# Larger scratch writes for the split state-space operands and a later, spread-out load of small inputs in a two-layer hybrid decoder

## The chip, the cores and the metric

The program runs on one core of one Trainium2 chip. The core has a matrix engine (PE; its weight loads are shown as PEld), a vector engine (DVE), an activation engine (ACT), a general engine (POOL) and a queue engine (SP); 16 DMA engines move data for all of them. DMAs are issued here from SP (weights, output) and from POOL (all else). The metric is the device time of one execution in microseconds (us).

## The reference

Two decoder layers over 256 tokens of width 2048, all in float32. Cut to what matters here:

```python
for l in range(2):
    q, k, v, u = x @ w_in[...]                # u: 1024 wide, 64 groups of 16
    attn = diff_attention(rope(q), rope(k), v)
    # state space: bu = einsum('blgh,gph->blgp', u, bb), complex, 64 states a group
    # scanned over the tokens; y = Re(C s) + D u; g = gelu(y); g * sigmoid(g @ w_glu)
    ssm = s5_ssm(u, ...)
    merged = sigmoid(x @ w_ga) * (attn @ w_attn_up) + sigmoid(x @ w_gs) * (ssm @ w_ssm_up)
    x = layer_norm(alpha * x + merged @ w_out)
    x = layer_norm(alpha * x + relu(x @ w_up)**2 @ w_down)
```

## The kernel before

Each float32 product is made of reduced-precision products. An operand is split into hi (a rounded copy, ACT, L142) and lo (the rest, DVE, L144), and PE adds hi·hi, hi·lo and lo·hi. Weights are streamed: SP loads one chunk of 128x1024 numbers (512 KB) into one of four buffers (L344), ACT and DVE split it into one of three hi/lo buffers, PE consumes it. `gemm_feat` (L536) uses 24 matmuls of 256 columns a chunk, `gemm_tok` (L480) 12 of 512 columns.

A layer goes: u (two `gemm_feat` of 8 chunks each), q, k, v, the gates, `w_attn_up`, GLU (`w_glu`), `w_ssm_up`, `w_out`, layer norm, MLP, layer norm. Beside this foreground a background of generators is advanced: after each chunk `bg.pump(rate[0])` adds credit (about microseconds of DVE work) and runs generator steps until it is spent. In layer 0 the background first runs `rope_gen` (rotary tables), `b_gen(0)` (state-space parameters and the split of B), then `ssm_gen`, and later attention beside it. For layer 1, `b_gen(1)` runs in layer 0's MLP through `ahead_gen`. `bg.finish(sgen)` (L995) runs whatever is left before GLU. A scheduler then orders the instructions of each engine by a simulated timeline; each engine takes its own in that order.

Two helpers tie POOL's DMAs to PE: a DMA in `drip` is issued one a chunk, behind the chunk's last matmul (L460); `hold` (L454) keeps an instruction behind the latest chunk.

The state space's input product needs B and u split and stacked on partitions. Both go through scratch in DRAM: `b_gen` writes hi, lo, hi for each of four groups (L606, 12 writes of 256 KB a layer into `bsplit`), `u_evac` writes hi, hi, lo of each pair of column tiles (L950, 12 writes of 256 KB a layer into `usplit`). `operands` (L674) reads them back, 96 partitions each, two DMAs a set, 16 sets a layer; there is one buffer each (`bs`, `us`), so a set's DMAs wait until PE has done the matmuls of the set before (L702). Six DVE operations follow on each set, and after four sets of a group come scan, output product `y` (L748), GELU.

The seven small inputs are loaded by POOL at the very start (L180 to L192). The last layer norm's reciprocal root for the second half of the tokens runs on POOL (L852).

Of the kernel before, what the change touches and what calls it, by code (L numbers as in the profile page):

```python
# [30 lines left out]
L = 64  # L31
NCH = S // L
# [8 lines left out]
RATE = (2.0, 1.8)  # L41
# [3 lines left out]
LEAD = 3  # L45
# [59 lines left out]
def trunk(ctx: ExitStack, tc: tile.TileContext, A, out):  # L105
    nc = tc.nc
    V, SC, GP, PE = nc.vector, nc.scalar, nc.gpsimd, nc.tensor
# [5 lines left out]
    tmp = ctx.enter_context(tc.tile_pool(name="tmp", bufs=1))  # L113
# [62 lines left out]
    dram = ctx.enter_context(tc.tile_pool(name="dram", bufs=1, space=bass.MemoryType.DRAM))  # L176
    xkeep = A["x"].rearrange("(t p) d -> t p d", p=P)
    x = [None, None]
    prm = slot([P, 3, 64], name="prm")
    GP.dma_start(prm, A["ssm_p"])  # L180
    pos_i = t_bg([P, S]).bitcast(I32)
    GP.dma_start(pos_i, A["pos"][None, :].broadcast_to([P, S]))
    inv = const([P, 2], "inv")
    GP.dma_start(inv, A["inv"])
    lnp = const([P, DEPTH, 2, 2, NKT], "lnp")
    GP.dma_start(lnp, A["lnp"])
    dsk = const([P, DEPTH, 8], "dsk")
# [215 lines left out]
    rate = [RATE[0]]  # L403
    wts = {}

    def weights(key, l, *idx):
        k = (key, l) + idx
        if k not in wts:
            wts[k] = A[key][(l,) + idx]
        return wts[k]  # L410

    for l in range(DEPTH):
# [11 lines left out]
        for key, *idx in order:  # L424
            w = weights(key, l, *idx)
# [3 lines left out]
    for c in range(4):  # L429
        raw = wpool.tile([P, 4, 256], F32, tag="w", name=nm("xraw"), bufs=RAW_BUFS)  # L430
        t = slot([P, 4, 2, 256], F32R, "xT")
        xT.append(t)
        parts = [slice(0, 2), slice(2, 4)] if c == 0 else [slice(0, 4)]
        for i, k in enumerate(parts):
            nc.sync.dma_start(raw[:, k], A["xT"][c][:, k])
            split(t[:, k, 0, :], t[:, k, 1, :], raw[:, k])
            if c + i < LEAD:
# [151 lines left out]
    def b_gen(l):  # L589


        raw = slot([P, 4, 2, 256], name="braw")
        for g in range(4):
            hold(GP.dma_start(raw[:, g], A["bT"][l][:, g]))
            yield 0.3
        if l == 0:
            yield from ssm_param_gen()
        else:
            yield 2.0
        bsplit[l] = dram.tile([4, 4, 3, 32, 2, 256], F32, tag=f"bsplit{l}", name=f"bsplit{l}")  # L600
        hi, lo = (slot([P, 4, 2, 256], name="bhl") for _ in range(2))
        for g in range(4):
            h = SC.activation(hi[:, g].bitcast(F32R), raw[:, g], AF.Copy)
            hold(h)
            V.tensor_tensor(lo[:, g].bitcast(F32R), raw[:, g], hi[:, g], op=ALU.subtract)
# [54 lines left out]
    def ssm_gen(l, st):  # L660
        lp = l * 32
        e_re = slot([P, 4, 8, L], name="e_re")
        e_im = slot([P, 4, 8, L], name="e_im")
        w = [slot([P, NCH, 8, L], name="sw") for _ in range(2)]
        for g in range(4):
            if l in emem:
                for t, e in zip((e_re, e_im), emem[l]):
                    drip.append((t[:, g], e[:, g]))
            else:
                for step in e_steps(l, g, e_im[:, g], e_re[:, g]):  # L670
                    yield 0.1 if isinstance(step, tuple) else step
        while st["u"] is None:
            yield 0.5
        def operands(i):  # L674
            if i == 16:
                return None
            g, h, kk = i // 4, i // 2 % 2, i % 2
            bs = tmp.tile([96, 2, 2, P], F32, tag="bs", name=nm("bs"), bufs=1)
            GP.dma_start(bs.rearrange("p q c s -> p q (c s)"), bsplit[l][g, 2 * kk:2 * kk + 2, :, :, h].rearrange("q m r s -> (m r) q s"))
            us = tmp.tile([96, 2, 256], F32, tag="us", name=nm("us"), bufs=1)  # L680
            GP.dma_start(us, st["split"][2 * kk:2 * kk + 2, :, :, 2 * g + h].rearrange("q m r t -> (m r) q t"))
            return bs, us

        nxt = operands(0)
        uT = st["u"]
        for g in range(4):
            jj = slice(lp + 8 * g, lp + 8 * g + 8)
            cz = tmp.tile([P, 2, 8, 32], F32, tag="cz", name=nm("cz"), bufs=2)
            GP.dma_start(cz, cmem[l][g] if l in cmem else A["cT"][l, g])
# [7 lines left out]
            for k in range(4):  # L697
                bs, us = nxt
                bu = psa.tile([P, 2, 2, NCH, L], F32, tag="bu", name=nm("bu"), bufs=1)
                for q in range(2):  # L700
                    for ri in range(2):
                        PE.matmul(bu[:, q, ri].rearrange("p a b -> p (a b)"), bs[:, q, ri, :].bitcast(F32R), us[:, q, :].bitcast(F32R), start=True, stop=True)  # L702
                nxt = operands(4 * g + k + 1)
                yield 0.3
                er = e_re[:, g, 2 * k:2 * k + 2, None, :].broadcast_to([P, 2, NCH, L])
                ei = e_im[:, g, 2 * k:2 * k + 2, None, :].broadcast_to([P, 2, NCH, L])
                wr, wi = (w[ri][:, :, 2 * k:2 * k + 2, :].rearrange("p c q t -> p q c t") for ri in range(2))
# [214 lines left out]

        return evac

    prep = [rope_gen(), b_gen(0)]
    first = True

    for l in range(DEPTH):
# [112 lines left out]
        norms = {}  # L1041
# [154 lines left out]
```

## Time and profile before

| | |
|---|---|
| Median of 3 runs | 2718.39 us (2705.3 to 2719.93) |
| Profiled execution, its own time | 2716.07 us |
| Its span | 2714.1 us |
| DVE, ACT, POOL busy | 70%, 48%, 5% |
| Mean granted PE clock | 0.992 of full speed |
| Moved by DMA | 535.76 MB, mean 197 GB/s |

Busy time is per engine over the span. "Idle before, releaser" says how long the engine waited ahead of an instruction and for whom. An "x" behind a busy time counts instructions; a few per cent of the matmul records can be missing. The granted clock is a share of PE's 2.4 GHz.

### The profile page before, as it was taken

To read this page: it belongs to the slowest core of one execution; us is meant where nothing else is said; L and a number is where in the kernel's file an instruction comes from. 1 tells how busy PE (TensorE), PEld (TensorE's weight loads), DVE (VectorE), ACT (ScalarE), POOL (GpSimd) and SP (SyncE) were. 2 spreads that over 40 slices of the span, in tenths; PEclk is the share of its full clock that TensorE was granted. 3 is DMA by queue.
4 is the path that set the end of the run, shared out by engine and by line. 5 is a ranking of instruction groups with operands and counts; after the bars stand their busy time and mean duration, and the time that the engine had idled before them with its cause. 6 is when DMAs were issued, how large, how long until landed. Compare 5 with 4: busy or idle time off the path is not lost. (4 is left out here: it accounts for less than half of the span.)

```text
span 2714.1 us, 37124 instructions
## 1 busy us (share of the span) xinstructions
PE 2648.8 (98%) x14144; PEld 2254.0 (83%) x14144; DVE 1906.6 (70%) x2675; ACT 1307.5 (48%) x1755; POOL 147.1 (5%) x274
## 2 busy tenths in 40 slices
PE   6999999999999999999998999999999999999998
PEld 6988877888888878888898987778888888888886
DVE  6899998666765566665656999987776655656556
ACT  4555555444554454443443655544445544435442
POOL 2100000000000010000012000001000000000000
PEclk9999999999999999999999999999999999999999
DMA  8756655674656677666657566557746666665673
GB/s 267 214 181 188 191 180 170 217 238 129 214 188 193 200 231 216 219 201 194 233 172 229 180 187 190 177 159 230 259 134 207 188 194 189 192 194 186 194 242 131
DMA packets 158659, 535.76 MB, mean 197 GB/s; under 512 B 27505, under 2 KB 27537, under 8 KB 158481
## 3 DMA queue, kind: packets, MB, share of 16 engines
q1 hardware_dynamic: 133344, 482.40, 56.1%
q0 software_dynamic: 25136, 50.99, 6.6%
q8 instruction: 111, 1.82, 0.3%
q14 instruction: 68, 0.55, 0.1%
HBM read 513.32 MB, written 19.92 MB: 196 GB/s over the span
## 5 line engine op out<-in xcount | busy, mean ns | idle before, releaser
L144 DVE TENSOR_TENSOR wlo<-w,whi 128x1024 fp32r<-128x1024 f32 (+1 forms) x884 | 1077.2, 1220 | 648.0 <-ACT whi L142 643.4
L142 ACT ACTIVATE whi<-w 128x1024 fp32r<-128x1024 f32 (+1 forms) x884 | 934.4, 1058 | 1073.8 <-PE g L478 649.9
L572 PE MATMUL g<-xT,whi 128*128 128x512 f32 x1920 | 656.3, 395 | 3.3 <-ACT whi L142 3.3
L572 PE MATMUL g<-xT,wlo 128*128 128x256 f32 x1920 | 497.9, 280 | 1.5 <-DVE wlo L144 1.5
L572 PEld LDWEIGHTS g<-xT,whi 128*128 128x128 f32 x1920 | 345.1, 188 | 68.2 <-ACT whi L142 3.9
L572 PEld LDWEIGHTS g<-xT,wlo 128*128 128x128 f32 x1920 | 362.2, 189 | 23.1 <-DVE wlo L144 2.8
L475 PE MATMUL g<-wlo,hT 128*128 128x512 f32 x972 | 378.2, 389 | 0.0
L474 PE MATMUL g<-whi,hT 128*128 128x512 f32 x972 | 378.2, 389 | 0.0
L478 PE MATMUL g<-whi,hT 128*128 128x512 f32 x972 | 299.1, 389 | 0.0
L475 PE MATMUL g<-wlo,xT 128*128 128x512 f32 x680 | 267.7, 394 | 0.5 <-DVE wlo L144 0.5
L474 PE MATMUL g<-whi,xT 128*128 128x512 f32 x680 | 265.5, 392 | 0.0
L549 PE MATMUL g<-xT,whi 128*128 128x256 f32 x768 | 218.6, 288 | 18.1 <-ACT whi L142 18.1
L551 PE MATMUL g<-xT,wlo 128*128 128x256 f32 x768 | 213.9, 289 | 5.6 <-DVE wlo L144 5.5
L550 PE MATMUL g<-xT,whi 128*128 128x256 f32 x768 | 218.1, 287 | 0.0
L475 PEld LDWEIGHTS g<-wlo,hT 128*128 128x128 f32 x972 | 182.5, 188 | 38.0
L474 PEld LDWEIGHTS g<-whi,hT 128*128 128x128 f32 x972 | 182.4, 188 | 37.9
L478 PEld LDWEIGHTS g<-whi,hT 128*128 128x128 f32 x972 | 182.4, 188 | 37.8
L478 PE MATMUL g<-whi,xT 128*128 128x512 f32 x680 | 211.5, 391 | 0.0
L549 PEld LDWEIGHTS g<-xT,whi 128*128 128x128 f32 x768 | 150.7, 196 | 19.1 <-ACT whi L142 19.0
L551 PEld LDWEIGHTS g<-xT,wlo 128*128 128x128 f32 x768 | 147.4, 197 | 7.8 <-DVE wlo L144 7.5
L550 PEld LDWEIGHTS g<-xT,whi 128*128 128x128 f32 x768 | 150.9, 197 | 0.0
L475 PEld LDWEIGHTS g<-wlo,xT 128*128 128x128 f32 x680 | 128.0, 188 | 27.3 <-issue 1.2
(292 smaller groups left out, 3162.9 us busy)
## 6 DMA issues: line engine op xcount, KB each, us to landing
w<-in_w_in_dram SPq DMA_DIRECT2D x253, 512.0 KB, 3.7
w<-in_w_mlp_down_dram SPq DMA_DIRECT2D x243, 512.0 KB, 3.5
w<-in_w_mlp_up_dram SPq DMA_DIRECT2D x240, 512.0 KB, 3.6
w<-in_w_out_dram SPq DMA_DIRECT2D x54, 512.0 KB, 4.5
w<-in_w_attn_up_dram SPq DMA_DIRECT2D x32, 512.0 KB, 3.6
w<-in_w_ssm_up_dram SPq DMA_DIRECT2D x32, 512.0 KB, 3.8
w<-in_w_glu_dram SPq DMA_DIRECT2D x16, 512.0 KB, 3.6
lnb<-in_ln_dram POOLq DMA_DIRECT2D x32, 256.0 KB, 4.1
```

Of the source, the lines that this page charges most:

```text
L142: SC.activation(hi, src, AF.Copy, scale=scale)
L144: V.tensor_tensor(lo, src, hi.bitcast(F32), op=ALU.subtract)
L474: mm(PE.matmul(ps[tt], act(kt)[:, 0, ts], hi[:, k, :], start=kt == 0, stop=False))
L475: mm(PE.matmul(ps[tt], act(kt)[:, 0, ts], lo[:, k, :], start=False, stop=False))
L478: mm(PE.matmul(ps[tt], act(kt)[:, 1, ts], hi[:, k, :], start=False, stop=kt == nkt - 1))
L549: m(PE.matmul(o, wh, ah, start=first and b % 2 == 0, stop=False))
L550: m(PE.matmul(o, wh, al, start=False, stop=False))
L551: m(PE.matmul(o, wl, ah, start=False, stop=last and b % 2 == 1))
L572: mm[j](PE.matmul(o, wt, mv, start=kt == 0 and i == 0, stop=last and i == 1))
```

## The change

The scratch gets another layout. B's hi and lo of two groups are gathered in one tile and written by one DMA of 1 MB (two a layer), and so are u's hi and lo of one `gemm_feat` (two a layer). The three stacked copies are no longer made in DRAM: `operands` reads 128 partitions (both of B's parts against both of u's, so lo·lo is added too), by four DMAs of 64 partitions a set, with B's rows repeated in the read. A set now holds another pair of the group's eight tiles (`k::4`).

The small inputs go into `drip`: one behind each of the first chunks. The first x tile is loaded in three pieces. `b_gen(0)` comes ahead of `rope_gen` and pauses for 4.0 credit; the rate is 1.2 instead of 2.0 in the two u products of layer 0. C's tiles are loaded one group ahead and under `hold`. The last layer norm's reciprocal root goes to DVE.

```diff
-    GP.dma_start(prm, A["ssm_p"])
...
-    GP.dma_start(lqk.rearrange("p a b c d -> p (a b c d)"), A["lqk"][None, :].broadcast_to([P, DEPTH * 4 * QK]))
...
-        parts = [slice(0, 2), slice(2, 4)] if c == 0 else [slice(0, 4)]
+        parts = [slice(0, 1), slice(1, 2), slice(2, 4)] if c == 0 else [slice(0, 4)]
...
-    drip = []
+    drip = [(prm, A["ssm_p"]), (pos_i, A["pos"][None, :].broadcast_to([P, S])), (inv, A["inv"]),
+            (lqk.rearrange("p a b c d -> p (a b c d)"), A["lqk"][None, :].broadcast_to([P, DEPTH * 4 * QK])),
+            (dsk, A["dsk"]), (sub, A["sub"]), (lnp, A["lnp"])]
...
+        if l == 0:
+            yield 4.0
...
-        hi, lo = (slot([P, 4, 2, 256], name="bhl") for _ in range(2))
-        for g in range(4):
...
-            for m, t in enumerate((hi, lo, hi)):
-                GP.dma_start(bsplit[l][g, :, m], t[:, g])
-            yield 0.6
+        bsplit[l] = [dram.tile([4, 32, 2, 2, 2, 256], F32, tag=f"bsplit{l}{i}", name=f"bsplit{l}{i}") for i in range(2)]
+        for i in range(2):
+            hl = slot([P, 2, 2, 2, 256], name="bhl")
...
+            GP.dma_start(bsplit[l][i].rearrange("j r m k h c -> (j r) (m k h c)"), hl.rearrange("p m k h c -> p (m k h c)"))
...
-            GP.dma_start(bs.rearrange("p q c s -> p q (c s)"), bsplit[l][g, 2 * kk:2 * kk + 2, :, :, h].rearrange("q m r s -> (m r) q s"))
-            GP.dma_start(us, st["split"][2 * kk:2 * kk + 2, :, :, 2 * g + h].rearrange("q m r t -> (m r) q t"))
+            for m in range(2):
+                ms = slice(64 * m, 64 * m + 64)
+                GP.dma_start(bs[ms].rearrange("p h c s -> p (h c s)"), b[m][:, None].broadcast_to([32, 2, 512]))
+                GP.dma_start(us[ms].rearrange("p h t -> p (h t)"), u)
...
-    prep = [rope_gen(), b_gen(0)]
+    prep = [b_gen(0), rope_gen()]
...
-            for m, t in enumerate((hi, hi, lo)):
-                GP.dma_start(st["split"][:, m, :, ct:ct + 2], t)
+            if b == 1:
+                GP.dma_start(st["split"][n].rearrange("j r m c t -> (j r) (m c t)"), uhl[n].rearrange("p m c t -> p (m c t)"))
...
+            rate[0] = 1.2 if l == n == 0 else RATE[l]
...
-                            lambda tt, vd: ln_stats(tt, stats, norms, vd, tt == 1))
+                            lambda tt, vd: ln_stats(tt, stats, norms, vd, tt == 1 and nxt is not None))
```

On POOL, in layer 0's u products, the order before was this (`bhl` and `uhl` are the split tiles, `bs` and `us` the operands of the state space's product):

```order
L594 DMA braw_317<-in_bT_dram 128x512 x4
L607 DMA bsplit_506<-bhl_507 4x32x512 x2
L607 DMA bsplit_506<-bhl_508 4x32x512
L951 DMA usplit_170<-uhl_168 4x32x512 x2
L607 DMA bsplit_506<-bhl_507 4x32x512 x2
L951 DMA usplit_170<-uhl_168 4x32x512 x2
L951 DMA usplit_170<-uhl_169 4x32x512
L607 DMA bsplit_506<-bhl_507 4x32x512 x4
```

After the change, at the same place on POOL:

```order
L459 DMA lnp<-in_lnp_dram 128x128
L959 DMA usplit_166<-uhl_164 128x2048
L604 DMA bsplit_538<-bhl_540 128x2048
L689 DMA us_1019<-usplit_166 64x512 x2
L604 DMA bsplit_539<-bhl_576 128x2048
L688 DMA bs_1018<-bsplit_538 64x1x512 x2
L959 DMA usplit_167<-uhl_165 128x2048
L688 DMA bs_1072<-bsplit_538 64x1x512
L689 DMA us_1073<-usplit_166 64x512
```

Four writes led by 128 partitions stand where 24 led by a dimension of 4 stood, and a set of operands takes four DMAs.

On PE, the output product `y` of layer 0's last group stood among the matmuls of `w_attn_up` (`ahl` is the attention's result), with some 12 chunks of it still to come:

```order
L478 MATMUL g_4546<-whi_4527,ahl_2593 128x512 x2
L748 MATMUL y_4257<-sw_605,cz_3728 32x256 x4
L474 MATMUL g_4545<-whi_4549,ahl_2593 128x512
L748 MATMUL y_4257<-sw_606,cz_3728 32x256 x4
L748 MATMUL y_4257<-sw_605,cz_3728 32x256 x4
L748 MATMUL y_4257<-sw_606,cz_3728 32x256 x4
L475 MATMUL g_4545<-wlo_4550,ahl_2593 128x512
```

After the change the same product stands within GLU (`ghl` is GELU's result split; `ghl_4790` its first half, which the last group doesn't touch):

```order
L546 MATMUL g_4798<-ghl_4790,wlo_4803 128x256
L756 MATMUL y_4368<-sw_745,cz_2659 32x256 x4
L544 MATMUL g_4799<-ghl_4790,whi_4802 128x256
L545 MATMUL g_4799<-ghl_4790,whi_4802 128x256
L546 MATMUL g_4799<-ghl_4790,wlo_4803 128x256
L544 MATMUL g_4799<-ghl_4790,whi_4802 128x256
L545 MATMUL g_4799<-ghl_4790,whi_4802 128x256
L546 MATMUL g_4799<-ghl_4790,wlo_4803 128x256
L756 MATMUL y_4368<-sw_746,cz_2659 32x256 x4
L756 MATMUL y_4368<-sw_745,cz_2659 32x256 x4
L756 MATMUL y_4368<-sw_746,cz_2659 32x256 x4
```

So the state space of layer 0 ends some 190 matmuls later in PE's order. Behind this piece PE has 28 more matmuls on the first half before the first one that reads the second.

## Rows read from the trace of the kernel before

**Rows 1.** The page: busy time of PE, and its busy tenths in 40 slices.

```profile
PE 2648.8 (98%) x14144; PEld 2254.0 (83%) x14144; DVE 1906.6 (70%) x2675; ACT 1307.5 (48%) x1755; POOL 147.1 (5%) x274
...
PE   6999999999999999999998999999999999999998
```

**Rows 2.** Busy time by stretch: PE, PEld, DVE, ACT, POOL, clock, DMA share, GB/s.

```profile
0.00:30.00 30.00, 19.03 (x131) 17.33 (x132) 19.34 (x49) 15.32 (x17) 9.05 (x24) 1.00 0.86 282
10.00:20.00 10.00, 6.58 (x48) 5.77 (x48) 7.29 (x14) 5.82 (x7) 0.00 (x0) 1.00 0.92 316
30.00:50.00 20.00, 20.00 (x168) 20.00 (x168) 19.44 (x67) 11.72 (x17) 6.25 (x9) 1.00 0.86 251
50.00:100.00 50.00, 35.29 (x251) 34.54 (x250) 28.09 (x46) 20.00 (x27) 13.13 (x20) 0.83 0.84 247
...
100.00:450.00 350.00, 347.39 (x1981) 291.41 (x1980) 336.21 (x575) 190.11 (x322) 19.64 (x35) 1.00 0.60 184
1430.00:1470.00 40.00, 30.57 (x231) 30.22 (x231) 20.29 (x24) 13.24 (x16) 9.68 (x15) 0.87 0.80 244
...
960.00:990.00 30.00, 25.18 (x129) 20.57 (x128) 19.93 (x28) 17.42 (x26) 4.32 (x7) 0.94 0.82 242
```

**Rows 3.** Waits, 0 to 115 us: total us, times, longest.

```profile
ACT whi L142 <- DMA w<-in_w_in_dram: 30.5, 11, 13.1
...
PE g L551 <- DVE wlo L144: 3.5, 4, 1.9
```

**Rows 4.** Waits, 1425 to 1475 us (layer 1's u products).

```profile
ACT whi L142 <- DMA w<-in_w_in_dram: 20.5, 4, 11.0
...
PE bu L702 <- DMA us<-usplit: 9.4, 2, 7.8
```

**Rows 5.** DMA issues of the whole span: count, KB each, median us to landing.

```profile
bsplit<-bhl POOLq DMA_DIRECT2D x24, 256.0 KB, 15.1
usplit<-uhl POOLq DMA_DIRECT2D x24, 256.0 KB, 12.5
bs<-bsplit POOLq DMA_DIRECT2D x32, 192.0 KB, 4.3
...
emem<-ss POOLq DMA_DIRECT2D x8, 256.0 KB, 4.4
xkeep<-x POOLq DMA_DIRECT2D x8, 256.0 KB, 10.5
...
cz<-in_cT_dram POOLq DMA_DIRECT2D x4, 256.0 KB, 7.2
...
lqk<-in_lqk_dram POOLq DMA_DIRECT2D x1, 256.0 KB, 7.8
ss<-in_pos_dram POOLq DMA_DIRECT2D x1, 128.0 KB, 7.1
```

**Rows 6.** Tile bs: ns min, median, max of an issue on POOL.

```profile
L679 POOL DMA_DIRECT2D bs<-bsplit x32: 637/640/674, 70.6 to 1738.6; - x32
```

**Rows 7.** Chain of waits near the end: start, us, two 512-column matmuls.

```profile
2641.90 0.45 PE g L478 x2
```

**Rows 8.** Timeline around layer 0's last `y`: start, us, instruction (DVE, then ACT).

```profile
443.46 0.68 DVE L737 TENSOR_TENSOR sw<-sw,ss 128x512 f32<-128x512 f32 x1
...
448.22 0.69 DVE L755 TENSOR_TENSOR ss<-y,ss 128x512 f32<-128x512 f32 x1
...
453.25 1.22 DVE L146 SCALAR_TENSOR_TENSOR ghl<-uT,ghl 128x1024 fp32r<-128x1024 f32 x1
...
451.95 1.07 ACT L142 ACTIVATE ghl<-uT 128x1024 fp32r<-128x1024 f32 x1
```

**Rows 9.** DVE timeline of the last layer norm.

```profile
2692.11 0.16 DVE L854 TENSOR_TENSOR rsp<-rstd 128x1 f32<-128x1 f32 x1
...
2694.07 2.73 DVE L1127 SCALAR_TENSOR_TENSOR x<-x,mv,lnb 128x512 f32<-128x512 f32 x4
...
2707.80 2.74 DVE L1129 SCALAR_TENSOR_TENSOR x<-x,rstd,lnb 128x512 f32<-128x512 f32 x4 [2.20 <-POOL rstd L856]
```

More of the change, by code (lines that the diff above doesn't have):

```diff
@@ L436, in trunk @@
             split(t[:, k, 0, :], t[:, k, 1, :], raw[:, k])
-            if c + i < LEAD:
+            if (c, i) in ((0, 0), (0, 2), (1, 0), (2, 0)):
                 load_next(c == i == 0)
@@ L599, in b_gen @@
             yield 2.0
-        bsplit[l] = dram.tile([4, 4, 3, 32, 2, 256], F32, tag=f"bsplit{l}", name=f"bsplit{l}")
-        hi, lo = (slot([P, 4, 2, 256], name="bhl") for _ in range(2))
-        for g in range(4):
-            h = SC.activation(hi[:, g].bitcast(F32R), raw[:, g], AF.Copy)
-            hold(h)
-            V.tensor_tensor(lo[:, g].bitcast(F32R), raw[:, g], hi[:, g], op=ALU.subtract)
-            for m, t in enumerate((hi, lo, hi)):
-                GP.dma_start(bsplit[l][g, :, m], t[:, g])
-            yield 0.6
+        bsplit[l] = [dram.tile([4, 32, 2, 2, 2, 256], F32, tag=f"bsplit{l}{i}", name=f"bsplit{l}{i}") for i in range(2)]
+        for i in range(2):
+            hl = slot([P, 2, 2, 2, 256], name="bhl")
+            for k in range(2):
+                hold(SC.activation(hl[:, 0, k].bitcast(F32R), raw[:, 2 * i + k], AF.Copy))
+                V.tensor_tensor(hl[:, 1, k].bitcast(F32R), raw[:, 2 * i + k], hl[:, 0, k], op=ALU.subtract)
+                yield 0.6
+            GP.dma_start(bsplit[l][i].rearrange("j r m k h c -> (j r) (m k h c)"), hl.rearrange("p m k h c -> p (m k h c)"))
     def e_steps(l, g, im, re, hold=lambda i: i):
@@ L664, in ssm_gen, with load_c @@
         w = [slot([P, NCH, 8, L], name="sw") for _ in range(2)]
+        def load_c(g):
+            cz = tmp.tile([P, 2, 8, 32], F32, tag="cz", name=nm("cz"), bufs=2)
+            hold(GP.dma_start(cz, cmem[l][g] if l in cmem else A["cT"][l, g]))
+            return cz
         for g in range(4):
@@ L671, in ssm_gen @@
                     yield 0.1 if isinstance(step, tuple) else step
+        cz_next = load_c(0)
         while st["u"] is None:
@@ L676, in operands @@
                 return None
-            g, h, kk = i // 4, i // 2 % 2, i % 2
-            bs = tmp.tile([96, 2, 2, P], F32, tag="bs", name=nm("bs"), bufs=1)
-            GP.dma_start(bs.rearrange("p q c s -> p q (c s)"), bsplit[l][g, 2 * kk:2 * kk + 2, :, :, h].rearrange("q m r s -> (m r) q s"))
-            us = tmp.tile([96, 2, 256], F32, tag="us", name=nm("us"), bufs=1)
-            GP.dma_start(us, st["split"][2 * kk:2 * kk + 2, :, :, 2 * g + h].rearrange("q m r t -> (m r) q t"))
+            g, j = i // 4, i % 4
+            bs = tmp.tile([P, 2, 2, P], F32, tag="bs", name=nm("bs"), bufs=1)
+            us = tmp.tile([P, 2, 256], F32, tag="us", name=nm("us"), bufs=1)
+            b = bsplit[l][g // 2][j, :, :, g % 2].rearrange("r m h c -> m r (h c)")
+            u = st["split"][g // 2][j, :, :, 2 * (g % 2):2 * (g % 2) + 2].rearrange("r m h t -> (r m) (h t)")
+            for m in range(2):
+                ms = slice(64 * m, 64 * m + 64)
+                GP.dma_start(bs[ms].rearrange("p h c s -> p (h c s)"), b[m][:, None].broadcast_to([32, 2, 512]))
+                GP.dma_start(us[ms].rearrange("p h t -> p (h t)"), u)
             return bs, us
@@ L687, in ssm_gen @@
             jj = slice(lp + 8 * g, lp + 8 * g + 8)
-            cz = tmp.tile([P, 2, 8, 32], F32, tag="cz", name=nm("cz"), bufs=2)
-            GP.dma_start(cz, cmem[l][g] if l in cmem else A["cT"][l, g])
+            cz = cz_next
+            cz_next = load_c(g + 1) if g < 3 else None
             rt = t_bg([P, 8, L])
@@ L704, in ssm_gen @@
                 yield 0.3
-                er = e_re[:, g, 2 * k:2 * k + 2, None, :].broadcast_to([P, 2, NCH, L])
-                ei = e_im[:, g, 2 * k:2 * k + 2, None, :].broadcast_to([P, 2, NCH, L])
-                wr, wi = (w[ri][:, :, 2 * k:2 * k + 2, :].rearrange("p c q t -> p q c t") for ri in range(2))
+                er = e_re[:, g, k::4, None, :].broadcast_to([P, 2, NCH, L])
+                ei = e_im[:, g, k::4, None, :].broadcast_to([P, 2, NCH, L])
+                wr, wi = (w[ri][:, :, k::4, :].rearrange("p c q t -> p q c t") for ri in range(2))
                 ta, tb = t_bg([P, 2, NCH, L]), t_bg([P, 2, NCH, L])
@@ L940, in trunk @@
         uT = slot([P, 8, 256], name="uT")
-        uhl = [slot([P, 8, 256], name="uhl") for _ in range(2)]
-        st["split"] = dram.tile([4, 3, 32, 8, 256], F32, tag=f"usplit{l}", name=f"usplit{l}")
+        uhl = [slot([P, 2, 4, 256], name="uhl") for _ in range(2)]
+        st["split"] = [dram.tile([4, 32, 2, 4, 256], F32, tag=f"usplit{l}{i}", name=f"usplit{l}{i}") for i in range(2)]
         def u_evac(b, ps):
@@ L946, in u_evac @@
             u = uT[:, ct:ct + 2, :]
-            hi, lo = (t[:, ct:ct + 2, :] for t in uhl)
+            hi, lo = (uhl[n][:, m, 2 * b:2 * b + 2] for m in range(2))
             SC.activation(u, ps, AF.Copy)
             split(hi.bitcast(F32R), lo.bitcast(F32R), u)
-            for m, t in enumerate((hi, hi, lo)):
-                GP.dma_start(st["split"][:, m, :, ct:ct + 2], t)
+            if b == 1:
+                GP.dma_start(st["split"][n].rearrange("j r m c t -> (j r) (m c t)"), uhl[n].rearrange("p m c t -> p (m c t)"))
         rate[0] = RATE[l]
```

5 lines of the change are left out of this document (removed).

## The prediction

> **What bounds the kernel now.** I read the page's busy line and slices first, then busy time by stretch, the waits of the bad stretches, the DMA issues, and two pieces of the timeline. The reader is to see in [rows 1] that PE is busy 2648.8 of 2714.1 us: all waiting together is 65 us, 2.4%, and the first slice is the worst (6 where nearly all others have 9). The change leaves the matmuls as many as they were, so it can win only waits and what a lowered clock costs.
>
> [rows 2] say where. At full pace PE starts 168 matmuls in 20 us (30:50), 8.4 a us. Counted by that, 0:30 with 131 lost 30 - 15.6 = 14.4 us; 50:100 with 251 lost 20.1 us, part of it waiting, part at a granted clock of 0.83; in layer 1, 1430:1470 with 231 lost 12.5 us (clock 0.87). In layer 0's MLP, 960:990 was idle 4.8 us, and the clock of 0.94 costs 25.2 x 0.06 = 1.5 us more: 6.3 us. These four stretches hold 53 us. From 100 to 450 us PE lacks 2.6 us only, with DVE at 96%.
>
> The waits name the weights' transfers: in the first 115 us ACT waits 30.5 us for them, 13.1 at once [rows 3], and in layer 1 20.5 us, beside 9.4 us that PE waits for `us` read back from scratch [rows 4]. In just these stretches POOL sends the split parts. Their 256 KB take 15.1 and 12.5 us to land at the median, where `emem`, as large and also written to DRAM, takes 4.4 [rows 5].
>
> Two readings fit. `emem` is led by 128 partitions, the split parts by a dimension of 4, so they may use few engines; or they are merely written in a crowd: `xkeep`, led by 128 too, takes 10.5 us amid `usplit` [rows 5]. The Trainium skill ("DMA: Bandwidth & Descriptors", on why a DMA increments its semaphore by 16) says that a DMA runs on the largest number of engines up to 16 that divides the slowest dimension of both sides: 4 before, 16 now. The ratio 15.1 to 4.4 agrees, 10.5 for `xkeep` warns that part of it is crowding. By this rule alone the writes' stalls would all go, by crowding alone only the bytes count; the sums below stand without it.
>
> **The change part by part.**
>
> *Start.* Before, the small inputs and two C tiles go out with the first weights: `lqk` and `pos`, the two largest of seven, and two of `cz` are 896 KB, 0.92 MB [rows 5]. At 316 GB/s, the best 10 us shown [rows 2], they take 2.9 us, in a stretch in which PE lives from hand to mouth. Behind the first products they compete with weights still, but later. The lower rate and the pause take DVE work away from the weights' lo parts, for which PE waited 3.5 us [rows 3]; I count 2.6 of it. Together -5.5 us; bounds: -1 (all returns as the same bytes a little later) and -9.
>
> *Writes in layer 0.* 24 writes of 256 KB, 6.3 MB, become four of 1 MB, 4.2 MB. What is left of the 20.1 us? A chunk is 0.524 MB for 24 matmuls, 2.86 us, so the weights want 183 GB/s. With 4.2 MB of writes, 1.0 MB for the first two operand sets and 0.5 MB of C over some 45 us, 127 GB/s come on top: 310 GB/s. That is just below the best of 316; 30:50 shows 251. At 280 in between, 1.4 MB come late, 5 us; with a bit for the second C tile and the inputs moved here I leave 5.6 us: -14.5. Bounds: at 247 GB/s (50:100) 2.8 MB are late, 11.5 us, -8.5; all gone, -20.
>
> *Writes in layer 1.* One 256 KB transfer a chunk (the tables `e_re`, `e_im` and `xkeep`) stays. 12.5 us at 244 GB/s are 3.0 MB late; 1.05 MB fewer are written, 4.3 us. If the even deal gives half of the rest too, -8.5. Bounds -4 and -12.5.
>
> *Writes in layer 0's MLP.* Likewise 1.05 MB fewer at 242 GB/s is 4.3 us of the 6.3; -4.5, bounds -1 and -6.3.
>
> *Operand reads.* Each of 32 sets now takes four DMAs and 512 KB for two and 384 KB. 4.2 MB more lie in stretches where the DMA share is 0.60 [rows 2]: nothing. The latency counts more. An issue of 96 partitions costs 0.64 us [rows 6]; four of 64 partitions are not shown, at most 4 x 0.64 = 2.6 us, at least the 1.3 us of now; I take 2.2. With 4.3 us to land [rows 5] a set comes 6.5 us after the matmuls before it. In PE's new order the fewest matmuls between two sets are 36 of 512 columns, at 0.225 us each [rows 7] 8.1 us. The order before left as few as 24 such, 5.4 us against 1.3 + 4.3 = 5.6, and outside the crowded stretches PE hardly waited. Cost 0. If that cover is gone, PE waits with all weights' matmuls queued behind it; priced as a rival. The Trainium skill ("DMA: Bandwidth & Descriptors", "Rules for kernel authors") speaks against the split in halves: two transfers to disjoint partition halves serialize, and one of 128 partitions should be used. By it halves win no time over whole transfers; no run so far shows it, and the sum stays as it is, since it counts all four.
>
> *Later end of the state space.* The wider sets and the lower rate put layer 0's last `y` within GLU. Before, from the end of the last DVE step ahead of it (443.46 + 0.68) to the second half of `ghl` (453.25 + 1.22) went 10.3 us [rows 8], hidden under `w_attn_up`. Now 28 matmuls of 256 columns, 3.3 us, lie between, so PE can stand 7.0 us. Without the wait ahead of it, from 448.22 to ACT's part at 453.02 is 4.8 us, 1.5 uncovered. Between the two, nearer the longer, since three weight splits stand in between on DVE: +4.5. Bounds +1 and +10 (DVE some us late besides).
>
> *Tail.* POOL's part goes, for which DVE idled 2.20 us; nine DVE instructions take its place, 2694.07 - 2692.11 = 1.96 us in the first half [rows 9]. The four independent steps no longer run beside it: -0.2 us, bounds -0.3 and +0.3.
>
> *The rest.* The stride `k::4` and the two parts side by side leave every DVE and PE instruction its size; `rope_gen` behind `b_gen` is needed only at q. Nothing.
>
> Sum: -5.5 - 14.5 - 8.5 - 4.5 + 4.5 - 0.2 = -28.7. From the profiled execution's 2716.07 that is 2687.4; that execution lies 2.3 us under the median of 2718.39, so I say 2688.
>
> **The rivals.**
>
> *Only bytes count* (the crowd, not the deal). For: `xkeep`'s 10.5 us, 0.84 DMA share in 50:100. Against: 247 GB/s there is less than 316. Then layer 0 wins 2.1 MB less 0.5 of wider sets, 1.6 MB at 247, 6.5 us; layer 1 4.3, MLP 4.3, start 2.9; with GLU's 4.5 back that is -13.5: 2704.
>
> *DVE becomes the bound of layer 0.* DVE has 96% in 100:450; PE arriving 20 us sooner at GLU may find the state space undone. For: `y` ends in GLU now. Against: DVE idled 20 us of 50:100 and 10 of 0:30, and can use them too. If three quarters of layer 0's 20 us return, 2703.
>
> *Operands late (slower).* At every set within a group, 24 of 32, PE waits in its order for the fourth DMA. It decides once a set lands later than 8.1 us after the set before. If the four take turns and the last lands at 10 us instead of 6.5, each costs 1.9 us, 46 us: 2688 + 46 = 2734. Against: the median landing is 4.3 us even with the crowd in it.
>
> *The change doesn't act*: the writes still run on few engines. The destination is led by 128 now, as `emem`'s; I give it nothing of its own, it would end like the first rival.
>
> **How the numbers follow.** Forecast 0.68 (its own range 2674 to 2702), bytes only 0.17, DVE 0.09, operands late 0.06. A change of under 0.5%, 13.6 us, can't be told from none with this kernel, whose three runs differ by 14.6; the line is at 2704.8. Faster: 0.67 of the first, 0.10 of the second, 0.05 of the third, 0.82. Same: 0.01, 0.07, 0.04, 0.01: 0.13. Slower 0.05. All good bounds at once give 2718.4 - 47.1 = 2671, all bad ones 2718.4 - 4.2 = 2714, which leaves out the slower rival; 8 in 10 I put from 2671 to 2709.
>
> **What would show it.** 50:100 with over 370 matmuls, not 251, and a clock near 1.0; 0:30 with over 165. The four large writes land in under 10 us each, and no wait of ACT for `w` is over 5 us there; with waits over 5 us the first rival is right. 1430:1470 over 300 matmuls. A new wait of PE at GLU, 3 to 7 us, at some 460 us; over 12 us says DVE. PE waiting for `us` or `bs` at many sets of 200 to 450 us says the slower rival, and it would prove me wrong outright; so would no change of the stall in 50:100.

## The result and the profile after

The changed kernel takes 2682.70 us (median of 4 runs, 2679.49 to 2684.72), the kernel before in the same session 2712.07 (4 runs); the ratio is 0.989, 95% interval 0.9864 to 0.9915. The forecast was 2688, its range 2671 to 2709. The profiled execution took 2682.85 us, its span is 2681.1, 33.0 shorter than before's; the profiled execution of before was 4 us above the later median, so differences of the two profiles come out some 4 us larger than those of the medians.

The page of the profile after: PE's busy line and its slices.

```profile
PE 2642.8 (99%) x14144; PEld 2250.5 (84%) x14144; DVE 1909.8 (71%) x2685; ACT 1308.3 (49%) x1756; POOL 139.4 (5%) x289
...
PE   8999999999999999999999999999999999999998
```

All of PE's waiting is now 38 us, not 65 [rows 1], and the first slice is an 8, not a 6.

Busy time by stretch after (PE, PEld, DVE, ACT, POOL, clock, DMA share, GB/s), against [rows 2]:

```profile
0.00:30.00 30.00, 22.98 (x162) 22.17 (x163) 16.32 (x25) 14.60 (x16) 7.21 (x21) 1.00 0.87 289
...
50.00:100.00 50.00, 50.00 (x419) 50.00 (x418) 44.99 (x89) 32.06 (x42) 4.98 (x10) 1.00 0.79 262
100.00:450.00 350.00, 344.40 (x1844) 285.10 (x1843) 325.25 (x550) 183.23 (x311) 31.92 (x63) 1.00 0.62 187
...
960.00:990.00 30.00, 30.00 (x165) 25.91 (x164) 22.20 (x29) 18.39 (x26) 0.94 (x2) 1.00 0.64 198
1430.00:1470.00 40.00, 39.16 (x326) 38.96 (x326) 38.97 (x56) 23.00 (x29) 4.47 (x10) 1.00 0.59 187
```

Three of the four bad stretches are full or nearly so at a clock of 1.00: 419 matmuls for 251, 165 for 129, 326 for 231. 0:30 has 162 for 131. The work of the last two comes some 18 and 26 us earlier in the changed kernel, so the like stretches there are these, and they are as full (174 and 332 matmuls):

```profile
942.00:972.00 30.00, 30.00 (x174) 26.19 (x174) 21.99 (x28) 18.25 (x24) 1.66 (x3) 1.00 0.76 247
1404.00:1444.00 40.00, 39.80 (x332) 39.57 (x331) 31.93 (x43) 20.62 (x25) 10.82 (x22) 1.00 0.88 270
```

The DMA issues after (count, KB each, median us to landing), against [rows 5]:

```profile
us<-usplit POOLq DMA_DIRECT2D x64, 128.0 KB, 4.9
bs<-bsplit POOLq DMA_DIRECT2D x64, 128.0 KB, 4.7
...
usplit<-uhl POOLq DMA_DIRECT2D x4, 1024.0 KB, 6.3
bsplit<-bhl POOLq DMA_DIRECT2D x4, 1024.0 KB, 6.6
...
xkeep<-x POOLq DMA_DIRECT2D x8, 256.0 KB, 6.2
```

1 MB lands in 6.3 and 6.6 us where 256 KB took 12.5 and 15.1. `xkeep`, which was not changed, went from 10.5 to 6.2. It lies beside the split writes; run 1 below (few bytes, uneven writes) has 8.5 for it and run 2 (the bytes of before, even writes) 7.1, so both play a part, and the uneven deal the larger one.

The largest wait for weights in the first 115 us, against [rows 3] (total, times, longest):

```profile
ACT whi L142 <- DMA w<-in_w_in_dram: 12.6, 11, 3.2
```

12.6 us for 30.5, and none over 3.2. In layer 1's u products [rows 4] ACT no longer waits for `w` at all. Of the signs that the forecast named, three were missed: 0:30 has 162 matmuls and not over 165, one of the four writes of layer 0 took 10.2 us and not under 10, and the new wait in GLU is 1.5 us and not 3 to 7 (its rows are shown further down).

### The profile page after: what moved, and what is told of

Its sections match the earlier page's. It is cut to its first block, busy times and chain, and to the rows that moved or that the text cites. A ratio compares the mean times of both kernels' runs of the same rounds, so it can differ in the third digit from the quotient of the medians.

```text
span 2681.1 us, 37176 instructions
## 1 busy us (share of the span) xinstructions
PE 2642.8 (99%) x14144; PEld 2250.5 (84%) x14144; DVE 1909.8 (71%) x2685; ACT 1308.3 (49%) x1756; POOL 139.4 (5%) x289
## 5 line engine op out<-in xcount | busy, mean ns | idle before, releaser
L567 PEld LDWEIGHTS g<-xT,whi 128*128 128x128 f32 x1920 | 344.4, 188 | 64.1
L567 PEld LDWEIGHTS g<-xT,wlo 128*128 128x128 f32 x1920 | 361.5, 188 | 20.8 <-DVE wlo L144 0.3
L544 PEld LDWEIGHTS g<-xT,whi 128*128 128x128 f32 x768 | 149.0, 194 | 6.1 <-ACT whi L142 6.0
L469 PEld LDWEIGHTS g<-whi,xT 128*128 128x128 f32 x680 | 128.4, 189 | 27.0 <-ACT whi L142 2.1
L473 PEld LDWEIGHTS g<-whi,xT 128*128 128x128 f32 x680 | 127.4, 188 | 27.1 <-issue 0.4
```

What stands on the lines that cost most here:

```text
L469: mm(PE.matmul(ps[tt], act(kt)[:, 0, ts], hi[:, k, :], start=kt == 0, stop=False))
L473: mm(PE.matmul(ps[tt], act(kt)[:, 1, ts], hi[:, k, :], start=False, stop=kt == nkt - 1))
L544: m(PE.matmul(o, wh, ah, start=first and b % 2 == 0, stop=False))
L567: mm[j](PE.matmul(o, wt, mv, start=kt == 0 and i == 0, stop=last and i == 1))
```

## The experiments

Each run was timed in five rounds; the kernel before had 2711.1, 2710.2 and 2711.9 us beside the three groups of runs. Four marks will do for most of them, read from the tiles' first starts: the matmuls of the first 100 us, the first matmul on `ahl` (`w_attn_up`, attention's result) and on `sgl` (`w_ssm_up`, behind GLU: the end of layer 0's mixer but for its output products), and the span. The first shows the transfers, `ahl` to `sgl` the end of attention and of the state space. The mark `ahl` is not quite the same place everywhere: from it to `sgl` PE does 430 matmuls before, 421 or 422 in the changed kernel and in runs 1, 2, 6, 11 and 12, 440 in run 5, 447 or 448 in runs 4, 7 and 9, and 460 or 461 in runs 3, 8 and 10, where more of attention's matmuls come behind the first on `ahl`.

| kernel | matmuls to 100 us | DVE busy to 100 us | `ahl` | `sgl` | span | median us |
|---|---|---|---|---|---|---|
| before | 546 | 66.9 | 432.8 | 505.8 | 2714.1 | 2711 |
| changed | 745 | 81.2 | 414.4 | 488.1 | 2681.1 | 2682.7 |
| 1 uneven | 618 | 67.8 | 426.4 | 500.1 | 2716.6 | 2719.9 |
| 2 small even, spare copies | 742 | 80.9 | 412.3 | 486.1 | 2677.5 | 2680.7 |
| 3 start alone | 591 | 67.4 | 424.2 | 512.2 | 2709.0 | 2718.1 |
| 4 writes alone | 666 | 82.6 | 417.9 | 503.8 | 2696.4 | 2697.2 |
| 5 full rate, no pause | 723 | 80.8 | 416.3 | 495.6 | 2686.4 | 2692.2 |
| 6 `us` by one DMA, led by 2 | 722 | 78.7 | 455.3 | 528.6 | 2776.6 | 2777.8 |
| 7 writes alone, late `y` | 684 | 83.5 | 415.6 | 502.7 | 2695.0 | 2698.7 |
| 8 start alone, late `y` | 612 | 67.9 | 422.7 | 516.5 | 2715.3 | 2723.0 |
| 9 writes alone, DVE later | 666 | 82.2 | 417.6 | 496.0 | 2689.2 | 2690.3 |
| 10 start alone, DVE later | 600 | 67.5 | 423.6 | 520.0 | 2715.4 | 2723.1 |
| 11 `us` by one DMA, led by 64 | 739 | 80.6 | 412.7 | 484.8 | 2684.5 | 2685.2 |
| 12 pieces of 256 KB | 734 | 79.7 | 415.0 | 488.7 | 2683.9 | 2685.3 |

The profiled execution of run 3 was the shortest of its twelve, 2711.2 us, so its row shows less loss than its median. Those of runs 5, 8 and 10 too were the shortest, 4 to 6 us under their medians.

**The deal or the bytes (runs 1 and 2).** Run 1 takes the even deal away and keeps everything else:

```diff
-        bsplit[l] = [dram.tile([4, 32, 2, 2, 2, 256], ...
+        bsplit[l] = [dram.tile([4, 33, 2, 2, 2, 256], ...
-            GP.dma_start(bsplit[l][i].rearrange("j r m k h c -> (j r) (m k h c)"), ...
+            GP.dma_start(bsplit[l][i][:, :32].rearrange("j r m k h c -> j r (m k h c)"), ...
```

> The changed kernel with one thing altered: the scratch of each split part has 33 rows in place of 32 in its second dimension, so that the same eight writes of 1 MB are led by a dimension of 4 again and not by 128. Bytes, count and order stay. Theory (the even deal over the engines is what frees the weights' transfers): the large writes land in over 20 us instead of 6.3, the weights wait again in 50:100, in layer 0's MLP and around 1430:1470, and over two thirds of the gain goes: 2703 to 2725 us. Rival (only the bytes and the count of writes matter): within 4 us of the changed kernel's 2682.7, that is 2679 to 2687.

Measured: 2719.9 us, ratio to before 1.003 (1.0018 to 1.0042), as the theory had it. All of the gain is gone. The issues and two stretches of run 1:

```profile
usplit<-uhl POOLq DMA_DIRECT2D x4, 1024.0 KB, 20.3
bsplit<-bhl POOLq DMA_DIRECT2D x4, 1024.0 KB, 19.5
...
xkeep<-x POOLq DMA_DIRECT2D x8, 256.0 KB, 8.5
```

```profile
50.00:100.00 50.00, 42.06 (x323) 41.00 (x322) 34.95 (x82) 22.45 (x32) 6.92 (x12) 0.93 0.75 248
...
1430.00:1470.00 40.00, 27.59 (x199) 27.24 (x198) 22.00 (x28) 12.06 (x14) 11.27 (x21) 0.83 0.73 234
```

The same bytes land three times as late, and the stall at 1430:1470 is larger than before the change (199 matmuls for 231). Not all of it is the weights': in 1425:1475 PE waits 12.4 us for `us`, which is read back behind the late writes (9.4 before the change [rows 4]). Run 2 keeps the deal and gives the bytes and the count back:

```diff
-            GP.dma_start(bsplit[l][i].rearrange("j r m k h c -> (j r) (m k h c)"), ...
+                for m in range(2):
+                    GP.dma_start(bsplit[l][i][:, :, m, k].rearrange("j r h c -> (j r) (h c)"), ...
+                GP.dma_start(bspare[:, 2 * i + k], hl[:, 0, k].rearrange("p h c -> p (h c)"))
```

> The changed kernel with its eight writes of 1 MB made 48 of 256 KB, each led by 128 partitions; of every six pieces two go to a spare scratch that nobody reads, so that bytes and count are those of the kernel before and only the deal is the new one. Theory (the deal decides): nearly all of the gain stays, 2682 to 2690 us, 50:100 with over 390 matmuls. Rival (bytes and count decide): the 4.2 MB more cost what my sum took for them, 6.5 us in layer 0 and 4.3 each in layer 1 and in the MLP, 2696 to 2700 us, with 50:100 under 370 matmuls.

Measured: 2680.7 us, ratio 0.9888 (0.9875 to 0.9901), as the changed kernel and 1.3 us below the theory's range. Its 50:100:

```profile
50.00:100.00 50.00, 49.90 (x416) 49.69 (x415) 45.08 (x93) 31.78 (x42) 10.58 (x20) 1.00 0.88 301
```

So the DMAs moved 301 GB/s there, some 2.0 MB more than in the changed kernel, and PE didn't notice. The rival that only bytes count is out: what bytes and count cost is too little to be seen here, and the deal costs the whole gain.

**The start and the writes apart (runs 3 and 4).** Run 3 is the kernel before with `drip`, x in three pieces, pause, rate and order of the changed one; run 4 is the changed kernel without these:

```diff
+    GP.dma_start(prm, A["ssm_p"])
...
-        if l == 0:
-            yield 4.0
...
-    prep = [b_gen(0), rope_gen()]
+    prep = [rope_gen(), b_gen(0)]
...
-            rate[0] = 1.2 if l == n == 0 else RATE[l]
```

> The kernel before with the start part alone: the small inputs one by one behind the first products, x in three pieces at first, the pause, the lower rate in the first product and the B preparation ahead of the rotary tables; writes, scratch and operand reads stay those of before. Theory (the start is worth about 5.5 us by itself, and the crowd behind it stays): 2704 to 2709 us, 0:30 with over 155 matmuls, not 131. Rival (what the start wins is lost again in the crowd of uneven writes that follows): 0:30 as full, but 50:100 with fewer than 251 matmuls and the whole at 2710 to 2716 us.

> The changed kernel with the start part undone (small inputs sent with the first weights, the usual rate, no pause, the old order of the two preparations); the large writes, the wider operand sets and the C tiles one group ahead stay. Theory (start and writes add up): 2686 to 2691 us, 0:30 with some 130 matmuls, 50:100 with over 390. Rival (the start wins nothing in the end, since the state space sets the time at GLU): 2680 to 2684 us.

Measured: the start alone 2718.1 us, ratio 1.0026 (1.0014 to 1.0037), 7 us slower than before; the writes alone 2697.2, ratio 0.9944 (0.9932 to 0.9956). All four ranges were missed, both theories and both rivals. The parts don't add up: the start loses 7 us by itself and is worth 14.5 (2697.2 - 2682.7) on top of the even writes. The table says where. By 100 us the start alone has done 45 matmuls more than before and the writes alone 120, at 8.4 a us 5.4 and 14.3 us, just what the sum took for each. At `sgl` the one is 6.4 us behind, and the other only 2.0 ahead. Thirteen to fifteen us of lead go between the marks `ahl` and `sgl`. Before, run 4 and (below) run 9, from mark to mark:

```profile
432.80:505.80 73.00, 70.94 (x430) 60.92 (x429) 49.39 (x68) 33.66 (x48) 0.00 (x0) 1.00 0.59 180
417.90:503.80 85.90, 77.89 (x448) 65.68 (x447) 61.13 (x93) 36.50 (x51) 0.00 (x0) 0.94 0.50 158
417.60:496.00 78.40, 75.22 (x448) 63.99 (x447) 61.52 (x94) 36.08 (x51) 0.00 (x0) 1.00 0.57 174
```

Of run 4's 12.9 us, 4.3 are 18 more matmuls (75.22 - 70.94, since run 9 has the same ones at full clock) and are no loss; 5.9 are waiting (8.0 us idle for 2.1) and 2.7 the lower clock (77.89 - 75.22). Run 4 there, PE, ACT and DVE (start, us, instruction, in brackets the idle time and who ended it):

```profile
431.66 0.15 DVE L828 TENSOR_SCALAR ss<-ss 128x4 f32<-128x4 f32 x1
...
446.43 3.64 PE L759 MATMUL y<-sw,cz 128*32 128x256 f32 x32 [5.39 <-DVE sw L747]
446.89 0.16 DVE L334 SCALAR_TENSOR_TENSOR rs<-rsa,rs 128x4 f32<-128x4 f32 x1
447.09 1.14 ACT L833 ACTIVATE at<-aux,rs 128x128 f32<-128x128 f32 x4 [4.24 <-DVE rs L334]
...
451.88 0.75 DVE L842 SCALAR_TENSOR_TENSOR ahl<-aux,gsub,ahl 128x512 fp32r<-128x512 f32 x1 [1.05 <-ACT ahl L841]
```

PE waits for the last `y`, and attention's last norm is late too: its reciprocal root is a chain of DVE instructions of 0.16 us each that stretches from 431.66 to 446.89, since in DVE's order the state space's scans and the weights' splits stand between them. PE has come earlier, DVE has not: its last step on `sw` ends at 447.0 us, before at 444.1. It isn't short of time. By 100 us it has done 15.7 us of work more than before, by 450 us as much (82.6 + 322.0 and 66.9 + 336.2 us); between the two it waited for ACT's hi parts and for PE's `bu` and `aux`. What is late is what its order puts ahead of attention's steps. (In the kernel before PE came 15 us later to `ahl`, and its only wait over 0.8 us there was 1.3.)

**Moving `y` (runs 7 and 8).** My first theory was PE's order: the changed kernel has this `y` within GLU. `hold` and a delay put it behind `w_attn_up`, in run 7 for the writes alone, in run 8 for the start alone:

```diff
+            if l == 0 and g == 3:
+                yield 60.0
             yps = psa.tile([P, 2, 2, 256], F32, tag="bu", name=nm("y"), bufs=1)[:, 0]
...
-                        mm[j](PE.matmul(yps[32 * j:32 * j + 32, h, :], ...
+                        i = PE.matmul(yps[32 * j:32 * j + 32, h, :], ...
+                        mm[j](hold(i) if l == 0 and g == 3 else i)
```

> The run with the writes alone (2697.2 us), with one alteration: layer 0's last four-by-eight `y` matmuls stand behind the last chunk of `w_attn_up` in PE's order, just ahead of GLU, and not near its start, where PE waited 5.4 us for `sw` from DVE at 441 us and its clock fell. Theory (the start's worth in the changed kernel is above all the place that it gives `y` in PE's order): the wait and the low clock in 440:460 go, `ahl` to `sgl` takes 74 to 77 us and not 85.9, and most of the 14.5 us to the changed kernel comes back: 2683 to 2688 us. Rival (the start's worth is its transfers and its DVE time): no change, 2693 to 2698 us, with the wait moved to GLU or given back elsewhere.

> The run with the start alone (2718.1 us, uneven writes), with the same alteration of `y`. Theory (the 7 us that the start alone lost against the kernel before were lost where PE waited 5.7 us for `y`'s operand): 440:460 full, 2700 to 2709 us, which is faster than the kernel before by about what the sum took for the start. Rival (the start loses in the crowd of uneven writes): 2714 to 2720 us, as without it.

Measured: 2698.7 (ratio 0.9962, 0.9951 to 0.9973) and 2723.0 us (1.0055, 1.0034 to 1.0075). They lie 0.7 and 3 us above their rivals' ranges. The theory falls: the wait only moved. PE in run 7:

```profile
445.37 1.25 PE L841 MATMUL aux<-ident,at 128*128 128x128 f32 x4 [4.94 <-ACT at L836]
```

With `y` out of the way, PE waits at the same time for attention's last output, behind the same DVE. So it isn't the place of a matmul; it is what stands before attention's last steps on DVE.

**Pause and rate (run 5).**

```diff
-        if l == 0:
-            yield 4.0
...
-            rate[0] = 1.2 if l == n == 0 else RATE[l]
```

> The changed kernel without its pause of 4.0 and without the lower background rate in the first product; the small inputs still go one by one, and the even writes stay. Theory (pause and rate matter by the order that they give, and here `y` stands in the last third of `w_attn_up`, late enough): within 4 us of the changed kernel, 2679 to 2687 us, no wait of PE for `sw` over 2 us in 430:470. Rival (they save the waits for lo parts at the start, which my sum counted at 2.6 us and more): 2686 to 2692 us, with PE waiting for `wlo` 3 us more in the first 60 us.

Measured: 2692.2 us, ratio 0.9941 (0.9923 to 0.9959), 9.5 us over the changed kernel and, by the intervals, not to be told from run 4: the rival's number, just past its end, but hardly by the rival's way. No wait of PE for `sw` came, as the theory had it. PE waits 2.6 us for `wlo` in the first 100 us, 1.2 in the changed kernel; 1.9 us are lost at `ahl`, and 7.5 by `sgl`. In DVE's order 17 instructions on `sw` stand behind attention's last step in the changed kernel, 9 here, none in before and in runs 3 and 4; `ahl` to `sgl` takes 73.7, 79.3, and in runs 3 and 4 88.0 and 85.9 us.

**Moving DVE's work (runs 9 and 10).** This is the direct test: the last group's scans from chunk 1 on (run 10: chunk 2) go behind attention's end, in run 9 in the kernel with the writes alone, in run 10 in that with the start alone.

```diff
                 if c > 0:
+                    if l == 0 and g == 3 and c == 1:
+                        yield 48.0
                     for ri in range(2):
-                        V.tensor_tensor(carry[:, ri, :], carry[:, ri, :], ...
+                        i = V.tensor_tensor(carry[:, ri, :], carry[:, ri, :], ...
+                        if l == 0 and g == 3 and c == 1:
+                            hold(i)
```

> The run with the writes alone (2697.2 us) with the last three quarters of layer 0's last state-space group (the scans and products from chunk 1 on) put behind attention's end in DVE's order: 15 of its instructions on `sw` then stand behind the last step on `ahl`, where the changed kernel has 17, the run at full rate 9 and the run with the writes alone none. The start stays that of before. Theory (the start part's worth in the changed kernel is that its lower rate and pause shift this DVE work behind attention's end, since DVE is what PE waits for there): from the first matmul on `ahl` to the first on `sgl` go 73 to 78 us and not 85.9, and the whole takes 2684 to 2690 us. Rival (the worth lies in the first 100 us): 2694 us or more.

> The run with the start alone and uneven writes (2718.1 us) with the last half of that group put behind attention's end on DVE: 14 instructions on `sw` and not none. Theory: `ahl` to `sgl` takes 73 to 79 us and not 88.0, and the whole 2704 to 2711 us, so that the start is worth its few us by itself. Rival (the start loses elsewhere with uneven writes): 2714 us or more.

Measured: run 9 2690.3 us (0.9916, 0.9896 to 0.9935), 6.9 less than run 4; its longest execution (2691.0) is below run 4's shortest (2693.0). From `ahl` to `sgl` go 78.4 us. Both numbers lie 0.3 to 0.4 past the theory's ranges, and the time is below the rival's 2694. Run 4's and then run 9's 440:460:

```profile
440.00:460.00 20.00, 13.84 (x70) 9.17 (x69) 13.10 (x22) 7.77 (x13) 0.00 (x0) 0.74 0.19 67
```

```profile
440.00:460.00 20.00, 19.41 (x84) 15.23 (x83) 20.00 (x37) 7.45 (x7) 0.00 (x0) 1.00 0.58 184
```

The hole is gone, and with it the low clock. So 6.9 of the 14.5 us that the start is worth, about half, come from the order on DVE alone, without any change in the start. The rest, 7.6 us, fits the first 100 us, the rival's place: run 9 has 666 matmuls there for 745, 79 at 8.4 a us, 9.4 us. At `ahl` only 3.2 us of that show and at `sgl` 7.9, but PE idles 3.2 us between the marks in both kernels, at full clock; the 4.7 us between are 27 matmuls that the changed kernel does ahead of `ahl`. The changed kernel's 0:100, then run 9's:

```profile
0.00:100.00 100.00, 92.98 (x745) 92.17 (x746) 81.21 (x179) 61.60 (x79) 15.41 (x37) 1.00 0.84 280
```

```profile
0.00:100.00 100.00, 86.91 (x666) 85.60 (x667) 82.16 (x182) 58.15 (x75) 17.86 (x41) 0.98 0.80 264
```

Run 10 missed, and its rival's condition came out: 2723.1 us (1.0052, 1.0033 to 1.0071). With uneven writes PE waited 4.2 us for attention's `at` again and then 4.0 us for `ghl` in GLU, and in 500:520 it was busy for 15.9 us of 20. Attention's end did come sooner on DVE (its last step on `ahl` ends at 454.1 us, in run 3 at 462.5), but the half that was moved came very late. DVE's last step on `sw` in run 9, then in run 10:

```profile
468.15 0.68 DVE L752 TENSOR_TENSOR sw<-sw,ss 128x512 f32<-128x512 f32 x1
```

```profile
494.47 0.68 DVE L738 TENSOR_TENSOR sw<-sw,ss 128x512 f32<-128x512 f32 x1
```

So the test with uneven writes wasn't the like of run 9's. One might blame DVE's lack of work done early: with uneven writes it has done 67 to 68 us of work by 100 us in all five kernels, with even ones 79 to 84 in all nine. But run 1 speaks against that: it has 67.8 us too, with the changed kernel's order on DVE (17 instructions on `sw` behind attention's last step), and takes the changed kernel's 73.7 us from `ahl` to `sgl`. Why the start alone is 7 us slower than before is therefore not shown; runs 3, 8 and 10 only show where PE waits.

**The operand reads (runs 6 and 11).** Run 6 reads `us` by one DMA of 128 partitions, not two of 64:

```diff
-                GP.dma_start(us[ms].rearrange("p h t -> p (h t)"), u)
+            GP.dma_start(us.rearrange("p h t -> p (h t)"), u[None].broadcast_to([2, 64, 512]))
```

Run 11 does so too, with the dimension of the copies inside; the halves of `bs` then go to every other partition:

```diff
-                GP.dma_start(bs[ms].rearrange("p h c s -> p (h c s)"), ...
-                GP.dma_start(us[ms].rearrange("p h t -> p (h t)"), u)
+                GP.dma_start(bs[m::2].rearrange("p h c s -> p (h c s)"), ...
+            GP.dma_start(us.rearrange("p h t -> p (h t)"), u[:, None].broadcast_to([64, 2, 512]))
```

> The changed kernel with `us` read by one DMA of 128 partitions in place of two of 64, so that an operand set is three DMAs and not four; the bytes that land stay the same. Theory (the reads are covered by 8.1 us of matmuls, so that their count costs nothing): 2680 to 2684 us, PE's waits for `us` still 2 to 4 us in all. Rival (halves take turns, and sets arrive late because of them): `us` lands sooner than the 4.9 us of a half, and the whole comes down by 3 us or more, below 2680 us.

> The changed kernel with `us` read by one DMA of 128 partitions, as in the run that took 2777.8 us, but with the two equal copies as the inner dimension of the source (64 rows, each twice) and not as the outer one (2 times 64 rows); the rows of `bs` are interleaved to fit. Theory (a DMA led by 2 on its source goes through few engines, and nothing else was wrong with one DMA): `us` lands in under 6 us and not 10.2, and the whole takes 2678 to 2686 us. Rival (one DMA of 128 partitions from a broadcast source is slow as such): `us` takes over 8 us again, 2740 us or more.

Measured: run 6 2777.8 us (1.0247, 1.0225 to 1.0269), run 11 2685.2 (0.9899, 0.9881 to 0.9918). Both expectations of run 6 were wrong, by over 90 us; run 11's theory held. The issues of `us` in run 6, then PE's waits for them in the whole span, then the issues in run 11:

```profile
us<-usplit POOLq DMA_DIRECT2D x32, 256.0 KB, 10.2
```

```profile
PE bu L710 <- DMA us<-usplit: 56.2, 15, 7.9
```

```profile
us<-usplit POOLq DMA_DIRECT2D x32, 256.0 KB, 3.8
```

The same 256 KB in the same number of DMAs: led by 2 on the source 10.2 us, led by 64 3.8. The Trainium skill ("DMA: Bandwidth & Descriptors", "Rules for kernel authors") names just this: an outermost dimension of c copies holds the whole DMA to at most c engines. The trace agrees in direction, 2.7 times, not in proportion (16 to 2 engines would be 8). It also shows the forecast's slower rival at work: sets that land later than the 8.1 us of cover make PE wait, 56.2 us in 15 waits; the price of 46 us that I gave it was too low, since the kernel lost 95. In the two profiles 61 us of that are more waiting of PE in all, and 34 more busy time at a mean granted clock of 0.980, not 0.996. The Trainium skill's rule on halves in the same section (one transfer of 128 partitions rather than two) agrees with run 11, where the whole lands in 3.8 us and a half in 4.9, but the time is the same as the changed kernel's: landing is covered either way.

**A try for the fastest (run 12).** The eight writes as 32 of 256 KB, as in run 2, without the spare copies:

```diff
-                GP.dma_start(bspare[:, 2 * i + k], hl[:, 0, k].rearrange("p h c -> p (h c)"))
...
-            GP.dma_start(st["spare"][:, 2 * n + b], hi.rearrange("p c t -> p (c t)"))
```

> The changed kernel with its eight writes of 1 MB as 32 even ones of 256 KB, each sent as soon as it is computed, without the spare copies: a try for the fastest version. Theory (only the deal counts, neither size nor count): 2678 to 2684 us, the same as the changed kernel. Rival (larger is better): 2687 us or more, for four times as many issues on POOL.

Measured: 2685.3 us, ratio 0.9898 (0.988 to 0.9916), 1.3 us above the theory's range and below the rival's: the same as the changed kernel within the intervals. No run beats it by more than they allow; run 2 (0.9888) and it (0.989) can't be told apart.

## Why the prediction was right, term by term

- *Writes in layer 0, -14.5.* By 100 us run 4 is 14.3 us ahead of before, counted in matmuls, and run 1 shows that it is the deal. The 5.6 us left as late were there as well: in 50:100 run 4 has 365 matmuls, so it loses 50 - 365 / 8.4 = 6.5 us. In the changed kernel, with the start, that stretch is full, and run 2 moved some 2 MB more there for nothing. The term was right for the place; most of it was lost again between `ahl` and `sgl` (see the start and the sum).
- *Writes in layer 1, -8.5, and in layer 0's MLP, -4.5.* From `sgl` to the MLP's last chunk (first matmul on `whl`, 1346.4 before, 1320.5 after) the lead grew from 17.7 to 25.9 us, 8.2 for the 4.5 predicted; the stretch 960:990 explains 6.3 of it, and 1.9 I haven't traced. From there to the end it grew by 7.1 to 33.0, for 8.5 and the tail's 0.2 (from the last `x` plus `g` to the last step on DVE go 6.7 us and not 6.9). Together -15.3 for -13.2, and run 4, with the start undone, has the same gain behind `sgl`: (2714.1 - 505.8) - (2696.4 - 503.8) = 15.7.
- *Start, -5.5.* This step was mis-sized, and adding the terms failed. By 100 us the start alone has won 5.4 us; in the end it won nothing alone (+7) and 14.5 on top of the even writes. What I counted was transfers and 2.6 us of DVE work; some 7.6 of the 14.5 are of that kind, in the first 100 us, and 6.9 are the shift of DVE's work behind attention's end, which I had booked as a cost.
- *Later end of the state space, +4.5.* It had the wrong sign. The wait in GLU came, at the place predicted, but was small. DVE and then PE after:

```profile
464.56 0.68 DVE L745 TENSOR_TENSOR sw<-sw,ss 128x512 f32<-128x512 f32 x1
...
474.22 1.22 DVE L146 SCALAR_TENSOR_TENSOR ghl<-uT,ghl 128x1024 fp32r<-128x1024 f32 x1
```

```profile
469.37 0.38 PE L546 MATMUL g<-ghl,wlo 128*128 128x256 f32 x1 [0.19 <-DVE wlo L144]
473.10 0.39 PE L544 MATMUL g<-ghl,whi 128*128 128x256 f32 x1 [1.08 <-ACT whi L142]
474.05 0.51 PE L544 MATMUL g<-ghl,whi 128*128 128x256 f32 x2 [0.21 <-ACT ghl L142]
```

From the end of the last DVE step, 465.24, to the second half of `ghl`, 475.44, go 10.2 us, as long as the 10.3 before. But PE lost 1.5 us, not 4.5: behind the 28 matmuls that I counted as cover stand two that need only ACT's part and 20 more of the first half. And I asked only what the shift costs in GLU, not what would have waited without it: run 4 shows that, 8.6 us of waiting and lower clock between `ahl` and `sgl` beyond those of before.
- *Operand reads, 0.* An issue of a half took 0.54 us at the median (`bs`), and one of `us` 0.53, four together 2.14 for the 2.2 assumed, and PE waited 2.6 us for `us` once, at 112.7, and not again till 450. The row of issues:

```profile
L688 POOL DMA_DIRECT2D bs<-bsplit x64: 518/540/553, 52.4 to 1712.2; - x64
```

- *DVE as the bound of layer 0*, the rival at 2703: PE does wait for DVE, but for its order and not for the amount of its work. Run 9 shows it for run 4 (2697), and run 7 fits; in runs 3 and 8 PE waits at the same place, but run 10 didn't free it. In the changed kernel the lower rate and the pause move the work out of the way; that the two edits belong together was not seen.
- *The sum.* The three terms of layer 0's mixer made -15.5, and at `sgl` the lead is 17.7. That was in part luck, since two errors of one cause cancelled: the writes by themselves bring only 2.0 us to `sgl`, not 14.5, as attention's end on DVE doesn't follow, and what lets it follow I had booked as a loss of 4.5. By the marks at `sgl` the lead is 2.0 for the writes, 7.8 more by DVE's order (run 9) and 7.9 more by the rest of the start. What the earlier C tiles and the stride bring was not run by itself.

## What to carry to other kernels

Look at the outermost dimension of both sides of each DMA before its bytes: led by 4 in place of 128, the same writes cost this kernel its whole gain, while half as many bytes again, led by 128, cost nothing. When a stall goes and one engine comes earlier to the next stretch, ask what it waits for there, and what the order of the other engine puts ahead of that step. Here DVE had the time but had scans ahead of attention's last steps, and half of what the start is worth came from moving them. Parts of a change that aim at different places need not add: measure each alone and with the other.

## What the runs showed of the hardware

- 1 MB from 128 partitions to DRAM lands in 6.3 us led by 128 and in 20.3 led by 4, and what lies beside it lands later: `xkeep`, unchanged, in 6.2 and 8.5 us.
- 256 KB read with two copies as the outer dimension: 10.2 us, as the inner one 3.8. An issue of the former cost POOL 0.84 us, of the latter 0.62.
- In 50:60 of the changed kernel the DMAs moved 360 GB/s, above the 316 that I took as the best, with PE full:

```profile
50.00:60.00 10.00, 10.00 (x86) 10.00 (x85) 8.90 (x33) 4.27 (x5) 1.06 (x2) 1.00 1.02 360
```
